# Lower parts of the first four up-projection weights on DVE, and modulation work behind the last token transpose

## The chip, the cores and the metric

The kernel runs on one core of a Trainium2 chip. Its time is device microseconds of one execution, and the number compared is the median of the runs. PE is the matrix engine (PEld its weight loads), DVE the vector engine, ACT the scalar engine, POOL the general engine, and SP the engine that issues most of the loads.

## The reference

512 tokens of 1024 features pass through two blocks. The first adds an attention mix and then an MLP with squared ReLU; the second is modulated by a condition vector:

```python
x = x + jnp.einsum('bse,ed->bsd', mixed, w_out)            # first block
hn = rmsnorm(x, mlp_norm_g)
hid = jnp.square(jax.nn.relu(jnp.einsum('bsd,df->bsf', hn, w_up)))
x = x + jnp.einsum('bsf,fd->bsd', hid, w_down)
...
mod_x = (jax.nn.silu(c) @ w_mod[l] + b_mod[l])[:, None, :] # second block
mod_c = jax.nn.silu(c_ctx) @ w_mod[l] + b_mod[l]
...                                                        # pooling and neighbourhood attention -> mix_x
x = x + gt1 * _rmsnorm(mix_x, g_post_mix[l])
y_x = _sq_relu_mlp(_modulate(x, g_pre_mlp[l], sh2, sc2), w_mlp_in[l], w_mlp_out[l])
x = x + gt2 * _rmsnorm(y_x, g_post_mlp[l])
```

All of it is float32. `w_mod` is 1024 x 6144; its product with two vectors (the condition and that of the context) gives the six modulation rows. The hidden width of both MLPs is 4096.

## The kernel before, in words

Every float32 operand of a large product is held as two parts: hi, a rounded copy that ACT writes, and lo, the source less hi, which DVE (or POOL, where `eng` says so) subtracts. That pair of instructions is `split`, lines 147 and 148. `mm3` (lines 152 to 154) forms hi x hi, hi x lo and lo x hi. A lo part is therefore always behind its hi part, and the third of three matmuls needs it.

The stages that the change touches:

- The output projection of the first block, which works off the four token tiles. `evac1` adds the residual (`xa`, line 938), multiplies by the norm's gain (`xg`, line 940), and `split_T` has PE transpose the tile (line 216, `n_0t` to `n_3t`) and splits the result into `hT`, the right-hand side of the first MLP. Tokens 0 and 1 and then 2 and 3 form the two 256-column halves in which the first up-projections run (`m1up`, weights `m1u0`, `m1u1`, ...).
- The first MLP, `mlp`. `up(j)` takes a 128-column weight of `w_up` through `weights`, which loads it (raw ring `m1u`) and splits it into `m1u{j}h` and `m1u{j}l`, both 128x1024, in a ring of five. For j below `WPJ` = 4 POOL does the lo part (line 829), for all others DVE. The squared ReLU of the result is `m1re`, `m1sq`, `m1hid`.
- The modulation, `mods`, a generator that `mlp` advances through `extra` after each up-projection. For each of six column blocks it loads eight 128x1024 tiles of `w_mod` on SP's queue (line 893) into two buffers (`mod`), and for each tile DVE multiplies it by one column of the condition and accumulates: line 896 for the first of the eight, line 898 for the other seven. Blocks 0 and 1 do that for both vectors, so each tile has a pair of instructions there. The accumulated tile `macc` is split into `mh` and `ml`, and PE sums it over the partitions with a matrix of ones (`mp`, lines 910 and 911).
- The output projection of the second block, `dense_two`. `evac1` there writes `y` (line 1265), `post` adds it to the tokens (`xb`, line 1244, scaled by `ssy` that POOL computes), `mod_T` scales (`n_0x` to `n_3x`, line 232), transposes, applies the modulation (`n_0v` to `n_3v`, lines 241 and 243) and splits into `h2T`.
- The second MLP, `mlp_seven`, whose `up` (line 1317) has the same rule for its weights `m2u0` to `m2u3`.

A scheduler in the build sets the order of the instructions on each engine from the data dependences, its own model of durations and the order in which the code issues them. The engines then run their lists in order; an instruction that waits holds up all behind it on its engine.

Of the kernel before, what the change touches and what calls it, by code (L numbers as in the profile page):

```python
# [16 lines left out]
P = 128  # L17
# [3 lines left out]
KC = D // P  # L21
# [73 lines left out]
RB2 = 2  # L95
RBX = (1, 1)
KPS2 = (2, 0, 1, 3)
WPJ = 4
LOP = 0
OT = True  # L100
DT = False
# [28 lines left out]
class Build:  # L130
# [14 lines left out]
    def split(self, hi, lo, src, eng=None):  # L145

        self.nc.scalar.activation(out=hi, in_=src, func=AF.Copy)  # L147
        (eng or self.nc.vector).tensor_tensor(out=lo, in0=src, in1=hi.bitcast(F32), op=ALU.subtract)  # L148

    def mm3(self, out, lh, ll, rh, rl, start, stop):  # L150
        mm = self.nc.tensor.matmul
# [670 lines left out]
    def mlp(self, hT, w1, w2, evac, extra, name, G=8):  # L822

        nc = self.nc
        ac = nc.scalar.activation
        hq = {}

        def up(j):
            wh, wl = self.weights(f"{name}u{j}", [(0, self.kview(w1, 0, KC, j * P, P))], KC, P, eng=self.nc.gpsimd if j < WPJ else None)
            acc = self.ps("s", f"{name}up{j}")  # L830
            nsp = 2 if j < NSP else 1
            w = SEQ // nsp
            if j % 4 == 0:
                hq[j // 4] = self.hquad(f"{name}hid{j // 4}")
            qd = hq[j // 4]
            for sp in range(nsp):
                cols = slice(sp * w, (sp + 1) * w)
                for k in range(KC):
                    hqd = hT[k // 4]
                    self.mm3(acc[:, cols], wh[:, k, :], wl[:, k, :], hqd[:, k % 4, 0, cols], hqd[:, k % 4, 1, cols], k == 0, k == KC - 1)  # L840
            r = self.ep.tile([P, SEQ], F32, tag="relu", name=f"{name}re{j}", bufs=2)
            s = self.ep.tile([P, SEQ], F32, tag="sqr", name=f"{name}sq{j}", bufs=2)
            ac(out=r, in_=acc, func=AF.Relu)  # L843
            nc.vector.scalar_tensor_tensor(out=s, in0=acc, scalar=0.0, in1=r, op0=ALU.max, op1=ALU.mult)  # L844
            self.split(qd[:, j % 4, 0, :], qd[:, j % 4, 1, :], s)
# [24 lines left out]
    def mods(self):  # L870

        nc, a = self.nc, self.a
        ac = nc.scalar.activation
        ep = self.ep
        sc = ep.tile([P, 2, KC], F32, tag="silu", name="silu_c", bufs=1)
        se = ep.tile([P, 2, KC], F32, tag="silue", name="silu_e", bufs=1)
        nc.gpsimd.dma_start(out=sc[:, 0, :], in_=a["c_2"][0].rearrange("(k p) -> p k", p=P))
        nc.gpsimd.dma_start(out=sc[:, 1, :], in_=a["c_ctx_2"].rearrange("(k p) -> p k", p=P))
        ac(out=se, in_=sc, func=AF.Exp, scale=-1.0)
        nc.vector.tensor_scalar(out=se, in0=se, scalar1=1.0, scalar2=None, op0=ALU.add)  # L880
        nc.vector.reciprocal(out=se, in_=se)
        nc.vector.tensor_tensor(out=sc, in0=sc, in1=se, op=ALU.mult)
        ones = ep.tile([P, P], F32R, tag="ones", name="ones", bufs=1)
        nc.vector.tensor_scalar(out=ones, in0=self.ident, scalar1=0.0, scalar2=1.0, op0=ALU.mult, op1=ALU.add)

        todo = {0: [(0, None, 1), (1, None, 7)], 1: [(0, "g_pre_mix_2", 0), (1, "g_pre_mix_2", 6)], 2: [(0, "g_post_mix_2", 2)],
                3: [(0, None, 4)], 4: [(0, "g_pre_mlp_2", 3)], 5: [(0, "g_post_mlp_2", 5)]}
        yield
        for cb in range(6):
            accs = [ep.tile([P, D], F32, tag=f"macc{s}", name=f"macc{cb}{s}", bufs=1) for s, _, _ in todo[cb]]  # L890
            for k in range(KC):
                rw = ep.tile([P, D], F32, tag="mraw", name=f"mod{cb}{k}", bufs=2)
                nc.sync.dma_start(out=rw, in_=a["w_mod_2"][0, k * P:(k + 1) * P, cb * D:(cb + 1) * D])
                for s in range(len(accs)):
                    if k == 0:
                        nc.vector.tensor_scalar(out=accs[s], in0=rw, scalar1=sc[:, s, k:k + 1], scalar2=None, op0=ALU.mult)
                    else:
                        nc.vector.scalar_tensor_tensor(out=accs[s], in0=rw, scalar=sc[:, s, k:k + 1], in1=accs[s],  # L898
                                                       op0=ALU.mult, op1=ALU.add)
                yield  # L900
            for (s, gname, dst) in todo[cb]:
                ah = self.part("wh", f"mh{cb}{s}")
                al = self.part("wl", f"ml{cb}{s}")
                self.split(ah, al, accs[s])
                row = ep.tile([P, D], F32, tag="xr", name=f"mrow{cb}{s}", bufs=2)[0:1, :]
                nc.gpsimd.dma_start(out=row, in_=a["b_mod_2"][:, cb * D:(cb + 1) * D])
                for hf in range(2):
                    pt = self.ps("t", f"mp{cb}{s}{hf}")
                    cols = slice(hf * 512, hf * 512 + 512)
                    nc.tensor.matmul(out=pt, lhsT=ones, rhs=ah[:, cols], start=True, stop=False)  # L910
                    nc.tensor.matmul(out=pt, lhsT=ones, rhs=al[:, cols], start=False, stop=True)
                    nc.vector.tensor_tensor(out=row[:, cols], in0=pt[0:1, :], in1=row[:, cols], op=ALU.add)
                if gname:
                    gr = ep.tile([P, D], F32, tag="xr", name=f"grow{cb}{s}", bufs=2)[0:1, :]
                    nc.gpsimd.dma_start(out=gr, in_=a[gname])
                    nc.vector.scalar_tensor_tensor(out=row, in0=row, scalar=(1.0 if cb in (1, 4) else 0.0),  # L916
                                                   in1=gr, op0=ALU.add, op1=ALU.mult)
                nc.gpsimd.dma_start(out=self.modrows[dst:dst + 1, :], in_=row)  # L918
                yield
# [4 lines left out]
    def dense_one(self):  # L924
        nc, a = self.nc, self.a
# [10 lines left out]
        def evac1(half, t, acc):  # L936
# [5 lines left out]
            if half == 1:  # L942
                self.inv_rms(x[t], r2, t, f"r2_{t}", self.ep.tile([P, D], F32, tag="xr", name=f"xs{t}", bufs=2))
                nc.gpsimd.tensor_tensor(out=r2[:, t:t + 1], in0=r2[:, t:t + 1], in1=r2[:, t:t + 1], op=ALU.mult)
        self.out_proj(a["w_out"], self.mixT, evac1, "o1")
        self.banks(a=(0, 1, 2), t=(3, 4), s=(5, 6, 7))

        self.kc = self.xc.tile([P, 4, 2, 256], F32R, name="kc")
# [39 lines left out]
        for i in range(4):  # L988
            wh, wl = self.weights(f"wkc{i}", [(0, self.kview(w_in, 0, KC, 1024 + i * P, P))], KC, P)
# [288 lines left out]
    def mlp_seven(self, hT, w1, w2, y, gg, name):  # L1278
# [3 lines left out]
        nc = self.nc  # L1282
# [29 lines left out]
        def plain(j):  # L1312

            return hid[j % G // 2][:, j % 2 * 1024:j % 2 * 1024 + 1024].rearrange("p (x t) -> p x t", x=2)

        def up(j, st):
            wh, wl = self.weights(f"{name}u{j}", [(0, self.kview(w1, 0, KC, j * P, P))], KC, P, eng=nc.gpsimd if j < WPJ else None)
            acc = self.ps("s", f"{name}up{j}")
            nsp = 2 if j < NSP else 1
            w = SEQ // nsp  # L1320
            for sp in range(nsp):
                cols = slice(sp * w, (sp + 1) * w)
                for k in range(KC):
                    hqd = hT[k // 4]
                    self.mm3(acc[:, cols], wh[:, k, :], wl[:, k, :], hqd[:, k % 4, 0, cols], hqd[:, k % 4, 1, cols], k == 0, k == KC - 1)
            s = st[:, j % 2]
            ac(out=s, in_=acc, func=AF.Relu)
            nc.vector.scalar_tensor_tensor(out=s, in0=acc, scalar=0.0, in1=s, op0=ALU.max, op1=ALU.mult)  # L1328
            if j // G == NG - 1:
                self.split(plain(j)[:, 0], plain(j)[:, 1], s)  # L1330
            elif j % 2 == 0:
                hi, lo = parts_of(j % G // 2)
                self.split(hi[:, 0], lo[:, 0], s[:, 0:256])
# [77 lines left out]
        for half in range(2):  # L1411
# [8 lines left out]
            j = (NG - 1) * G  # L1420
# [30 lines left out]
```

## Time and profile before

| | us |
|---|---|
| median of 3 runs | 1255.92 |
| lowest, highest | 1253.18, 1258.51 |
| the profiled execution | 1260.07 |
| its span in the trace | 1258.3 |

Its mean granted clock of PE was 0.988 of full speed. The busy shares over the span are PE 96%, DVE 67%, ACT 45%, POOL 28%. A share is an average over stages with different limits; what a change at one place is worth is read from the timeline there. In a timeline the bracket at the end of a row is the time that the engine sat idle before the instruction, and what ended it. Rows with x2 or more join instructions of one kind that follow each other.

### The profile page before, as it was taken

How to read it: one execution, taken by the hardware profiler on the slowest of the kernel's cores; microseconds unless marked ns; L12 is line 12 of the kernel's file. 1: busy time of each engine (PE TensorE's matmuls, PEld its weight loads, DVE VectorE, ACT ScalarE, POOL GpSimd, SP SyncE). 2: the span in 40 equal slices, each digit the busy share in tenths (PEclk: the TensorE clock that was granted, in tenths of full speed). 3: DMA queues.
4: the chain of work that ended last, by engine and by line, in shares of the span. 5: the costliest groups of instructions: out<-in, count | busy, mean ns of one | idle time of the engine just before them, and what ended most of it. 6: DMA issues, size and time to landing. Idle time of an engine off the chain costs nothing. (4 is left out here: it accounts for less than half of the span.)

```text
span 1258.3 us, 16992 instructions
## 1 busy us (share of the span) xinstructions
PE 1213.5 (96%) x6316; PEld 1017.5 (81%) x6316; DVE 844.6 (67%) x1410; ACT 567.3 (45%) x1068; POOL 355.1 (28%) x370
## 2 busy tenths in 40 slices
PE   7899999999999999999999999999899999999997
PEld 6898888779888878888889878777798888888885
DVE  3799766597898854346355557574868678777744
ACT  5576656434223313225254546463546454343431
POOL 2787552252010000000014124030642504205502
PEclk9899999999999999999999999999999999999999
DMA  6222222365678734134145311215443643524421
GB/s 165 64 60 53 57 63 68 101 183 154 197 220 258 240 119 138 67 101 135 67 151 157 84 53 52 85 38 201 124 162 102 185 123 117 147 81 134 150 68 67
DMA packets 151707, 150.71 MB, mean 120 GB/s; under 512 B 14345, under 2 KB 115480, under 8 KB 151624
## 3 DMA queue, kind: packets, MB, share of 16 engines
q1 hardware_dynamic: 147224, 139.41, 36.4%
q0 software_dynamic: 4400, 10.22, 2.6%
q8 instruction: 49, 0.80, 0.3%
q14 instruction: 34, 0.28, 0.1%
HBM read 143.24 MB, written 6.36 MB: 119 GB/s over the span
## 5 line engine op out<-in xcount | busy, mean ns | idle before, releaser
L1365 POOL TENSOR_TENSOR m2d<-m2d,m2d 128x1024 f32<-128x1024 f32 x24 | 71.2, 2981 | 162.2 <-DVE m2w220l L148 51.5
L898 DVE SCALAR_TENSOR_TENSOR macc<-mod,silu_c,macc 128x1024 f32<-128x1024 f32 x56 | 76.1, 1369 | 15.5 <-DMA mod<-in_w_mod_dram 15.2
L975 DVE SCALAR_TENSOR_TENSOR xa<-m1d,r,xa 128x512 f32<-128x512 f32 x32 | 23.8, 746 | 37.5 <-PE m1d L154 37.5
L918 POOL DMA_DIRECT2D modrows<-mrow x8 | 3.9, 492 | 146.4 <-DVE mrow L916 91.9
L147 ACT ACTIVATE m2hid<-m2sq 128x512 fp32r<-128x512 f32 (+1 forms) x32 | 17.6, 551 | 49.1 <-DVE m2sq L1328 49.1
L147 ACT ACTIVATE m1hid<-m1sq 128x512 fp32r<-128x512 f32 x32 | 20.0, 630 | 38.3 <-DVE m1sq L844 38.3
L148 DVE TENSOR_TENSOR npl<-t,nph 128x512 fp32r<-128x512 f32 x32 | 21.7, 682 | 16.4 <-ACT nph L147 16.3
L194 POOL TENSOR_SCALAR p<-p,d 128x512 f32<-128x512 f32 x8 | 14.0, 1752 | 57.1 <-DVE d L1116 27.3
L148 DVE TENSOR_TENSOR m2hid<-m2sq,m2hid 128x512 fp32r<-128x512 f32 (+1 forms) x32 | 24.3, 760 | 6.0 <-ACT m2hid L147 5.8
L181 POOL TENSOR_SCALAR w<-w,g_attn 128x384 f32<-128x384 f32 x20 | 25.8, 1297 | 9.1 <-DMA w<-in_w_in_dram 6.7
L148 DVE TENSOR_TENSOR m1hid<-m1sq,m1hid 128x512 fp32r<-128x512 f32 x32 | 22.0, 687 | 9.1 <-ACT m1hid L147 9.1
L683 DVE TENSOR_REDUCE mb<-sb 128x1 f32<-128x128 f32 (+3 forms) x32 | 15.6, 487 | 16.5 <-PE sb L680 16.4
L1115 ACT ACTIVATE p<-s,m 128x512 f32<-128x512 f32 x32 | 22.0, 688 | 5.8 <-DVE m L1113 5.8
L1069 POOL TENSOR_TENSOR tb<-G,nam 128x256 f32<-128x256 f32 x24 | 17.8, 774 | 22.1 <-DVE m L1109 12.5
L685 ACT ACTIVATE pb<-sb,mb 128x128 f32<-128x128 f32 (+3 forms) x32 | 16.8, 525 | 16.0 <-DVE mb L683 15.7
L843 ACT ACTIVATE m1re<-m1up 128x512 f32<-128x512 f32 x32 | 18.6, 583 | 10.1 <-PE m1up L154 9.8
L204 POOL TENSOR_SCALAR nc_0ss<-nc_0ss 128x1 f32<-128x1 f32 x1 | 0.2, 187 | 80.5 <-ACT nc_0x L256 80.5
L152 PE MATMUL pj<-w_0h,xnT 128*128 128x384 f32 (+1 forms) x48 | 18.0, 376 | 4.9 <-ACT pjs L407 3.9
L147 ACT ACTIVATE nph<-t 128x512 fp32r<-128x512 f32 x32 | 19.0, 595 | 7.5 <-PE t L1126 7.2
L981 POOL DMA_DIRECT2D xspill<-xa x4 | 2.6, 655 | 70.0 <-DVE xa L975 69.9
L844 DVE SCALAR_TENSOR_TENSOR m1sq<-m1up,m1re 128x512 f32<-128x512 f32 x32 | 21.8, 683 | 0.1
L1328 DVE SCALAR_TENSOR_TENSOR m2sq<-m2up,m2sq 128x512 f32<-128x512 f32 x32 | 21.9, 684 | 0.0
(2017 smaller groups left out, 4679.7 us busy)
## 6 DMA issues: line engine op xcount, KB each, us to landing
mod<-in_w_mod_dram SPq DMA_DIRECT2D x48, 512.0 KB, 4.6
m2d<-in_w_mlp_out_dram SPq DMA_DIRECT2D x44, 512.0 KB, 3.7
m1u<-in_w_up_dram SPq DMA_DIRECT2D x32, 512.0 KB, 4.3
m1d<-in_w_down_dram SPq DMA_DIRECT2D x32, 512.0 KB, 3.6
m2u<-in_w_mlp_in_dram SPq DMA_DIRECT2D x32, 512.0 KB, 4.1
w<-in_w_in_dram SPq DMA_DIRECT2D x16, 512.0 KB, 4.2
w<-in_w_in_dram SPq DMA_DIRECT2D x48, 128.0 KB, 2.6
o1w<-in_w_out_dram SPq DMA_DIRECT2D x8, 512.0 KB, 3.8
```

Of the source, the lines that this page charges most:

```text
L147: self.nc.scalar.activation(out=hi, in_=src, func=AF.Copy)
L148: (eng or self.nc.vector).tensor_tensor(out=lo, in0=src, in1=hi.bitcast(F32), op=ALU.subtract)
L152: mm(out=out, lhsT=lh, rhs=rh, start=start, stop=False)
L181: eng.tensor_scalar(out=rv[:, i], in0=rv[:, i], scalar1=g, scalar2=None, op0=ALU.mult)
L843: ac(out=r, in_=acc, func=AF.Relu)
L844: nc.vector.scalar_tensor_tensor(out=s, in0=acc, scalar=0.0, in1=r, op0=ALU.max, op1=ALU.mult)
L898: nc.vector.scalar_tensor_tensor(out=accs[s], in0=rw, scalar=sc[:, s, k:k + 1], in1=accs[s], op0=ALU.mult, op1=ALU.add)
L975: nc.vector.scalar_tensor_tensor(out=x[t][:, cols], in0=acc, scalar=r2[:, t:t + 1], in1=x[t][:, cols], op0=ALU.mult, op1=ALU.add)
L1069: nc.gpsimd.tensor_tensor(out=tb[:, h, y], in0=G[:, h, ::-1, o:o + 32][:, :, ::-1], in1=nam[:, y, :].unsqueeze(1).to_broadcast([P, 8, 32]) ...
L1115: ac(out=pr, in_=s, func=AF.Exp, bias=m[:, 2:3], accum_out=den[:, 0:1])
L1328: nc.vector.scalar_tensor_tensor(out=s, in0=acc, scalar=0.0, in1=s, op0=ALU.max, op1=ALU.mult)
L1365: pt(out=o, in0=x, in1=z, op=ALU.subtract)
```

## The change

It has two parts. In both MLPs the rule that gave the lo parts of the first four weights to POOL is gone, so that DVE subtracts all of them. And in `mods`, the two instructions of column block 0 that multiply the first tile are issued behind `turned_in`, the last `split` of the first output projection, which is the lo part of token tile 3 in `hT`. Issued behind means that the scheduler may not place them ahead of it on DVE; the accumulations that follow depend on them and so move as well.

```diff
@@ -95,7 +95,6 @@
 RB2 = 2
 RBX = (1, 1)
 KPS2 = (2, 0, 1, 3)
-WPJ = 4
 LOP = 0
 OT = True
 DT = False
@@ -145,7 +144,7 @@
     def split(self, hi, lo, src, eng=None):
 
         self.nc.scalar.activation(out=hi, in_=src, func=AF.Copy)
-        (eng or self.nc.vector).tensor_tensor(out=lo, in0=src, in1=hi.bitcast(F32), op=ALU.subtract)
+        self.last_split = (eng or self.nc.vector).tensor_tensor(out=lo, in0=src, in1=hi.bitcast(F32), op=ALU.subtract)
 
     def mm3(self, out, lh, ll, rh, rl, start, stop):
         mm = self.nc.tensor.matmul
@@ -826,7 +825,7 @@
         hq = {}
 
         def up(j):
-            wh, wl = self.weights(f"{name}u{j}", [(0, self.kview(w1, 0, KC, j * P, P))], KC, P, eng=self.nc.gpsimd if j < WPJ else None)
+            wh, wl = self.weights(f"{name}u{j}", [(0, self.kview(w1, 0, KC, j * P, P))], KC, P)
             acc = self.ps("s", f"{name}up{j}")
             nsp = 2 if j < NSP else 1
             w = SEQ // nsp
@@ -893,7 +892,8 @@
                 nc.sync.dma_start(out=rw, in_=a["w_mod_2"][0, k * P:(k + 1) * P, cb * D:(cb + 1) * D])
                 for s in range(len(accs)):
                     if k == 0:
-                        nc.vector.tensor_scalar(out=accs[s], in0=rw, scalar1=sc[:, s, k:k + 1], scalar2=None, op0=ALU.mult)
+                        with self.tc.issue_after(self.turned_in.ins) if cb == 0 else nullcontext():
+                            nc.vector.tensor_scalar(out=accs[s], in0=rw, scalar1=sc[:, s, k:k + 1], scalar2=None, op0=ALU.mult)
                     else:
                         nc.vector.scalar_tensor_tensor(out=accs[s], in0=rw, scalar=sc[:, s, k:k + 1], in1=accs[s],
                                                        op0=ALU.mult, op1=ALU.add)
@@ -943,6 +943,8 @@
                 self.inv_rms(x[t], r2, t, f"r2_{t}", self.ep.tile([P, D], F32, tag="xr", name=f"xs{t}", bufs=2))
                 nc.gpsimd.tensor_tensor(out=r2[:, t:t + 1], in0=r2[:, t:t + 1], in1=r2[:, t:t + 1], op=ALU.mult)
         self.out_proj(a["w_out"], self.mixT, evac1, "o1")
+
+        self.turned_in = self.last_split
         self.banks(a=(0, 1, 2), t=(3, 4), s=(5, 6, 7))
 
         self.kc = self.xc.tile([P, 4, 2, 256], F32R, name="kc")
@@ -1314,7 +1316,7 @@
             return hid[j % G // 2][:, j % 2 * 1024:j % 2 * 1024 + 1024].rearrange("p (x t) -> p x t", x=2)
 
         def up(j, st):
-            wh, wl = self.weights(f"{name}u{j}", [(0, self.kview(w1, 0, KC, j * P, P))], KC, P, eng=nc.gpsimd if j < WPJ else None)
+            wh, wl = self.weights(f"{name}u{j}", [(0, self.kview(w1, 0, KC, j * P, P))], KC, P)
             acc = self.ps("s", f"{name}up{j}")
             nsp = 2 if j < NSP else 1
             w = SEQ // nsp
```

At the entry of the first MLP this stands in DVE's list before: the accumulations of the last two tiles of column block 0 among the token work (`xa`, `xg`, `hT` as above; `o` the projection's result).

```order
L898 SCALAR_TENSOR_TENSOR macc_3459<-mod_3668,silu_c,macc_3459 128x1024
L898 SCALAR_TENSOR_TENSOR macc_3460<-mod_3668,silu_c,macc_3460 128x1024
L940 TENSOR_TENSOR xg_3329<-xa_3022,g_mlp 128x512
L898 SCALAR_TENSOR_TENSOR macc_3459<-mod_3734,silu_c,macc_3459 128x1024
L898 SCALAR_TENSOR_TENSOR macc_3460<-mod_3734,silu_c,macc_3460 128x1024
L148 TENSOR_TENSOR hT_3031<-n_1t_3290,hT_3031 128x4x128
L938 TENSOR_TENSOR xa_3023<-o_3_3344,xa_3023 128x512
L148 TENSOR_TENSOR hT_3031<-n_2t_3331,hT_3031 128x4x128
L940 TENSOR_TENSOR xg_3370<-xa_3023,g_mlp 128x512
L148 TENSOR_TENSOR m1u4l<-m1u_3672,m1u4h 128x1024
L148 TENSOR_TENSOR hT_3031<-n_3t_3372,hT_3031 128x4x128
L148 TENSOR_TENSOR ml_3739<-macc_3459,mh_3738 128x1024
```

In the list now, at the same place, with block 0's first accumulations at the end:

```order
L147 TENSOR_TENSOR m1u1l<-m1u_3465,m1u1h 128x1024
L147 TENSOR_TENSOR m1u2l<-m1u_3534,m1u2h 128x1024
L938 TENSOR_TENSOR xa_3023<-o_3_3344,xa_3023 128x512
L940 TENSOR_TENSOR xg_3370<-xa_3023,g_mlp 128x512
L147 TENSOR_TENSOR hT_3031<-n_2t_3331,hT_3031 128x4x128
L147 TENSOR_TENSOR m1u3l<-m1u_3603,m1u3h 128x1024
L147 TENSOR_TENSOR m1u4l<-m1u_3672,m1u4h 128x1024
L147 TENSOR_TENSOR hT_3031<-n_3t_3372,hT_3031 128x4x128
L896 TENSOR_SCALAR macc_3459<-mod_3461,silu_c 128x1024
L896 TENSOR_SCALAR macc_3460<-mod_3461,silu_c 128x1024
L898 SCALAR_TENSOR_TENSOR macc_3459<-mod_3526,silu_c,macc_3459 128x1024
L898 SCALAR_TENSOR_TENSOR macc_3460<-mod_3526,silu_c,macc_3460 128x1024
```

What moved: the accumulations stand behind the last `hT` lo part, and the lo parts `m1u1l`, `m1u2l` and `m1u3l`, which were not in DVE's list, stand ahead of it. Between the last transposes `n_3t` and the first sum `mp` PE's list has 210 matmuls of 256 columns now, and had 177 before.

PE's list at the first sums of the modulation, before (`mp` with its two halves of columns, and up-projection 5 behind):

```order
L154 MATMUL m1up_3678<-hT_3031,m1u4l 128x256
L910 MATMUL mp_3744<-mh_3738,ones 128x512
L911 MATMUL mp_3744<-ml_3739,ones 128x512
L910 MATMUL mp_3748<-mh_3738,ones 128x512
L911 MATMUL mp_3748<-ml_3739,ones 128x512
L152 MATMUL m1up_3759<-hT_3030,m1u5h 128x512
L153 MATMUL m1up_3759<-hT_3030,m1u5h 128x512
```

And now:

```order
L153 MATMUL m1up_3678<-hT_3031,m1u4l 128x256
L910 MATMUL mp_3744<-mh_3738,ones 128x512
L910 MATMUL mp_3748<-mh_3738,ones 128x512
L151 MATMUL m1up_3759<-hT_3030,m1u5h 128x512
L152 MATMUL m1up_3759<-hT_3030,m1u5h 128x512
L911 MATMUL mp_3744<-ml_3739,ones 128x512
L911 MATMUL mp_3748<-ml_3739,ones 128x512
L151 MATMUL m1up_3817<-hT_3030,m1u6h 128x512
L152 MATMUL m1up_3817<-hT_3030,m1u6h 128x512
L153 MATMUL m1up_3759<-hT_3030,m1u5l 128x512
```

What moved: the two sums of `mh` come first, two matmuls of `m1up` with `m1u5h` stand between them and the sums of `ml`, and the first matmul with `m1u5l` follows two more with `m1u6h`.

DVE's list at the entry of the second MLP, before:

```order
L232 TENSOR_SCALAR n_0x<-xb_8441,ssx_8550 128x1024
L1244 SCALAR_TENSOR_TENSOR xb_8442<-y_8424,ssy_8435,xb_8442 128x512 x2
L1265 TENSOR_TENSOR y_8425<-o_2_8684,g_post 128x512
L243 TENSOR_SCALAR n_0v_8580<-n_0t_8575,g_mod_8429 128x128 x4
L232 TENSOR_SCALAR n_1x<-xb_8442,ssx_8647 128x1024
L148 TENSOR_TENSOR h2T_8432<-n_0v_8568,h2T_8432 128x4x128
L148 TENSOR_TENSOR h2T_8433<-n_0v_8580,h2T_8433 128x4x128
L1265 TENSOR_TENSOR y_8425<-o_2_8714,g_post 128x512
L243 TENSOR_SCALAR n_1v_8677<-n_1t_8672,g_mod_8429 128x128 x4
L148 TENSOR_TENSOR h2T_8432<-n_1v_8665,h2T_8432 128x4x128
L148 TENSOR_TENSOR h2T_8433<-n_1v_8677,h2T_8433 128x4x128
L1244 SCALAR_TENSOR_TENSOR xb_8443<-y_8425,ssy_8436,xb_8443 128x512 x2
```

And now, from `n_0v` on (`m2u0l` and `m2u1l` stand ahead of these rows):

```order
L242 TENSOR_SCALAR n_0v_8580<-n_0t_8575,g_mod_8429 128x128 x4
L231 TENSOR_SCALAR n_1x<-xb_8442,ssx_8647 128x1024
L147 TENSOR_TENSOR m2u2l<-m2u_9013,m2u2h 128x1024
L147 TENSOR_TENSOR h2T_8432<-n_0v_8568,h2T_8432 128x4x128
L147 TENSOR_TENSOR h2T_8433<-n_0v_8580,h2T_8433 128x4x128
L147 TENSOR_TENSOR m2u3l<-m2u_9072,m2u3h 128x1024
L1267 TENSOR_TENSOR y_8425<-o_2_8714,g_post 128x512
L242 TENSOR_SCALAR n_1v_8677<-n_1t_8672,g_mod_8429 128x128 x4
L1246 SCALAR_TENSOR_TENSOR xb_8443<-y_8425,ssy_8436,xb_8443 128x512 x2
L147 TENSOR_TENSOR m2u4l<-m2u_9138,m2u4h 128x1024
L147 TENSOR_TENSOR h2T_8432<-n_1v_8665,h2T_8432 128x4x128
L147 TENSOR_TENSOR h2T_8433<-n_1v_8677,h2T_8433 128x4x128
```

What moved: `m2u2l` stands ahead of the first token's `h2T` lo parts, and `m2u3l`, the pair `xb` of token tile 2 and `m2u4l` ahead of the second token's, where that pair and `m2u4l` were behind it.

## Rows read from the trace of the kernel before

**Rows 1.** Page, part 1: busy us (share of the span) xcount.
```profile
PE 1213.5 (96%) x6316; PEld 1017.5 (81%) x6316; DVE 844.6 (67%) x1410; ACT 567.3 (45%) x1068; POOL 355.1 (28%) x370
```

**Rows 2.** Timeline of PE, first MLP's entry: start, us, engine, line, op, idle before.
```profile
284.77 0.63 PE L216 MATMUL n_2t<-ident,xg 128*128 128x128 f32 x4 [3.15 <-DVE xg L940]
...
291.49 0.60 PE L216 MATMUL n_3t<-ident,xg 128*128 128x128 f32 x4
```

**Rows 3.** Windows: stretch, PE, PEld, DVE, ACT, POOL busy, granted clock, DMA share, GB/s.
```profile
285.00:289.00 4.00, 4.00 (x24) 4.00 (x23) 4.00 (x6) 1.43 (x3) 3.92 (x3) 0.57 1.03 292
296.00:345.00 49.00, 49.00 (x283) 42.95 (x283) 42.80 (x48) 18.95 (x26) 2.87 (x5) 1.00 0.55 165
345.00:420.00 75.00, 75.00 (x324) 60.69 (x323) 63.27 (x67) 22.66 (x27) 8.21 (x14) 1.00 0.75 236
446.00:449.00 3.00, 3.00 (x9) 2.32 (x8) 2.46 (x3) 1.30 (x2) 0.00 (x0) 0.50 0.26 101
906.00:910.00 4.00, 3.99 (x21) 3.99 (x22) 3.72 (x5) 3.51 (x10) 1.24 (x4) 0.59 0.17 62
```

**Rows 4.** Timeline of DVE, entry of the first MLP.
```profile
278.33 5.69 DVE L898 SCALAR_TENSOR_TENSOR macc<-mod,silu_c,macc 128x1024 f32<-128x1024 f32 x2
...
284.54 2.47 DVE L898 SCALAR_TENSOR_TENSOR macc<-mod,silu_c,macc 128x1024 f32<-128x1024 f32 x2
...
292.75 0.69 DVE L148 TENSOR_TENSOR hT<-n_3t,hT 128x512 fp32r<-128x512 f32 x1 [0.92 <-ACT hT L147]
...
306.59 0.75 DVE L896 TENSOR_SCALAR macc<-mod,silu_c 128x1024 f32<-128x1024 f32 x1
```

**Rows 5.** Timeline of POOL, the same stretch.
```profile
279.60 3.34 POOL L148 TENSOR_TENSOR m1u2l<-m1u,m1u2h 128x1024 fp32r<-128x1024 f32 x1
```

**Rows 6.** Timeline of PE, entry of the second MLP.
```profile
898.03 1.06 PE L216 MATMUL n_1t<-ident,n_1x 128*128 128x128 f32 x8 [1.35 <-DVE n_1x L232]
...
904.14 0.38 PE L152 MATMUL m2up<-h2T,m2u3h 128*128 128x256 f32 x1 [0.63 <-DVE y L1265]
906.01 0.39 PE L153 MATMUL m2up<-h2T,m2u1h 128*128 128x256 f32 x1 [1.49 <-DVE h2T L148]
```

**Rows 7.** Timeline of DVE, entry of the second MLP.
```profile
888.14 5.69 DVE L1244 SCALAR_TENSOR_TENSOR xb<-y,ssy,xb 128x512 f32<-128x512 f32 x2 [0.43 <-POOL ssy L1237]
895.26 0.69 DVE L1265 TENSOR_TENSOR y<-o,g_post 128x512 f32<-128x512 f32 x1 [1.42 <-ACT sj L1232]
...
898.12 5.37 DVE L148 TENSOR_TENSOR h2T<-n_0v,h2T 128x512 fp32r<-128x512 f32 x2 [0.23 <-ACT h2T L147]
...
906.66 1.41 DVE L1244 SCALAR_TENSOR_TENSOR xb<-y,ssy,xb 128x512 f32<-128x512 f32 x2
907.99 1.22 DVE L148 TENSOR_TENSOR m2u4l<-m2u,m2u4h 128x1024 fp32r<-128x1024 f32 x1
...
917.06 1.29 DVE L148 TENSOR_TENSOR h2T<-n_2v,h2T 128x512 fp32r<-128x512 f32 x2
```

**Rows 8.** Loads of line 893: issue to landing of 512 KB, us.
```profile
DMA to landing us min/median/max: 3.6/4.6/9.2
```

**Rows 9.** Timeline of PE, up to the first sums of the modulation.
```profile
307.23 0.28 PE L152 MATMUL m1up<-hT,m1u4h 128*128 128x256 f32 x1
...
312.93 0.39 PE L910 MATMUL mp<-mh,ones 128*128 128x512 f32 x1
313.16 0.40 PE L911 MATMUL mp<-ml,ones 128*128 128x512 f32 x1
```

**Rows 10.** Page, part 5: multiply-adds of line 898: count, busy, mean ns, idle before them.
```profile
L898 DVE SCALAR_TENSOR_TENSOR macc<-mod,silu_c,macc 128x1024 f32<-128x1024 f32 x56 | 76.1, 1369 | 15.5 <-DMA mod<-in_w_mod_dram 15.2
```

**Rows 11.** Timeline of all engines at a later sum of the modulation.
```profile
422.26 1.06 ACT L147 ACTIVATE mh<-macc 128x1024 fp32r<-128x1024 f32 x1 [2.18 <-DVE macc L898]
...
424.79 0.40 PE L911 MATMUL mp<-ml,ones 128*128 128x512 f32 x1
```

**Rows 12.** Timeline of PE, a wait for DVE later in the first MLP.
```profile
444.42 0.50 PE L152 MATMUL m1d<-m1d100h,m1hid 128*128 128x512 f32 x1 [1.81 <-DVE xa L975]
```

## The prediction

> **What bounds the kernel now.** I read the busy table first: PE is busy for 1213.5 of 1258.3 us, DVE for 844.6, POOL for 355.1 [rows 1]. So the time is PE's list, and work that moves between DVE and POOL counts only where PE waits for it, or where PE's clock is lower after such a wait. The second view is therefore PE's timeline at the two places the change touches. At the entry of the first MLP PE stands 3.15 us ahead of the transposes `n_2t`, until DVE has written `xg` [rows 2], and the stretch from 285 to 289 shows a granted clock of 0.57, near the 1.2 GHz level, against 1.00 at 2.4 GHz [rows 3]. At the entry of the second MLP it stands 1.35, 0.63 and 1.49 us, each time for DVE, and 906 to 910 shows 0.59 [rows 3, 6]. Third, DVE's timeline there. In the first MLP a pair of accumulations took 5.69 us where the next pair took 2.47 [rows 4]; in its time POOL ran `m1u2l`, 279.60 to 282.94 [rows 5]. In the second, one `xb` pair took 5.69 us and a later one 1.41, one `h2T` pair 5.37 and a later one 1.29 [rows 7]. The reader should see that DVE is not full but late, and that its slow pairs lie beside POOL's lo parts.
>
> **The change part by part.** Durations are of the execution of 1260.07 us (span 1258.3, and 1.8 around it), which lies 4.15 above the median of 1255.92. The sum is a difference, made there and carried to the median.
>
> *A, first entry.* The last `xg` no longer stands behind the slow pair: the accumulations are out of the token work, and POOL has no lo part to run beside it. What comes in is `m1u1l` to `m1u3l`, each 1.22 us by the row of `m2u4l` [rows 7]; one of them costs half of the pair that it replaces, so DVE is early for `xg`. The wait of 3.15 goes, and with it the low clock, 4 us x (1 - 0.57) = 1.7. Together -4.9. Bounds: 0, if lo parts that wait for ACT's hi parts hold `xg` as long, and -4.9.
>
> *B, second entry.* The waits are 1.35 + 0.63 + 1.49 = 3.47, the clock 4 x (1 - 0.59) = 1.6. On DVE 5.69 - 1.41 = 4.28 and 5.37 - 1.29 = 4.08 go. Five lo parts and an `xb` pair now stand ahead of the second token's `h2T` parts: 5 x 1.22 + 1.41 = 7.5. So these come 0.9 earlier if all stands back to back, and 2.9 if the lo parts fill the idle 0.43 + 1.42 + 0.23 [rows 7]. I take the middle, 1.9, and half of the clock, 0.8: -2.7. Bounds: -5.1, all waits and clock gone, and 0: the `xb` pair that is now ahead waits for POOL's `ssy`, and behind it on DVE are `m2u4l` and the `h2T` parts that PE waits for; a wait like the 0.43 in front of the pair at 888.14, twice, would take back the 0.9.
>
> *C, first sums of the modulation.* The moved accumulations now start behind the lo part of `n_3t`, which ended 292.75 + 0.69 - 291.49 = 1.95 us after the transposes began [rows 2, 4]. Two tiles are loaded by then; each later load starts only when one of the two buffers is free. With the median landing of 4.6 us [rows 8], 2.47 for a pair and 1.4 for the first pair (two of 0.75 that overlap a little) [rows 4]: tiles 0 and 1 are done at 1.4 and 3.9; tile 2 lands at 6.0 and is done at 8.5; tile 3 lands at 8.5, done at 11.0; tile 4 at 15.6, tile 5 at 18.1, tile 6 at 22.7, tile 7 at 25.2, the first vector's half of it at 24.0. ACT's hi part `mh` takes 1.06 [rows 11]. From the transposes: 1.95 + 24.0 + 1.06 = 27.0. The `m1sq` and `m1hid` instructions of the up-projections that stand between the pairs fit in the load waits in part; up to 1.9 more, or 28.9. What covers it on PE are the 210 matmuls of 256 columns between the transposes and the first sum. 48 such took 312.93 - 307.23 = 5.70 us [rows 9], so 24.9, and 0.4 for the transposes: 25.3. The new wait is 1.7 to 3.6; I take 2.7. The sums of `ml` and the first matmul with `m1u5l` follow one and two DVE lo parts behind; four and two matmuls at 0.23 [rows 9] lie between: 1.22 - 0.9 + 1.22 - 0.5 = 1.0. Behind a wait of this length the clock has been low (A), 1.7 more. C = +5.4. Queued behind the waiting `mp` is all of the first MLP, since PE's list is one line. Bounds: 0, where landings at the shortest, 3.6, take 3 x 1.0 off the chain (three load cycles stand in it); and 10.0, where one of them is the longest, 9.2.
>
> By the Trainium skill ("DMA: Bandwidth & Descriptors", "Anatomy of one DMA", fitted on the gpsimd path) a transfer takes about 2.0 us plus its bytes at 436 GB/s, an estimate of 3.2 us for 512 KB. By that figure C would be nothing and the sum -2.5; the trace does not agree, with 3.6 as its shortest landing and 4.6 as its median, under other traffic.
>
> *D, the later sums.* 2.47 x 7 + 1.4 = 18.7 us of DVE work moves behind 293. DVE was idle for 49.00 - 42.80 + 75.00 - 63.27 = 17.9 between 296 and 420 [rows 3], and 15.2 of the idle time before accumulations in the whole kernel was spent on loads [rows 10], which a later DVE no longer waits for. So it nearly fits, but with no room left: at the sum near 424.6 `mh` ended at 422.26 + 1.06, a lo part of 1.22 behind it ends at 424.54, and PE took `ml` at 424.79: 0.2 us to spare [rows 11]. Of four sums in this stretch (column blocks 1 to 4) I take two to be late by as much as the nearest wait for DVE, 1.81 [rows 12], and one of them with the clock that followed that wait, 3 x (1 - 0.50) = 1.5 [rows 3]: 5.1. Bounds: 0, and four times 1.81 + 1.5, 13.2. What leaves POOL beyond A and B is idle time there and worth nothing: in these rows only the `xb` pair waits for POOL, for `ssy`, which comes no later with less ahead of it.
>
> Sum: -4.9 - 2.7 + 5.4 + 5.1 = +2.9. Profiled 1263.0; on the median 1255.92 + 2.9 = 1258.8.
>
> **The rivals.** *Faster: the modulation stays hidden.* If loads land near 3.6 us, C is nothing and DVE reaches the later sums with its old lead: -7.6 with D at 0, -10.0 with B at its bound. For it: idle time of 17.9 for 18.7 of work, and the lead that block 0 had before: its accumulations stood ahead of the lo part at 292.75, 20 us ahead of the first sum at 312.93 [rows 4, 9]. Against it: 4.6 is the median, and the chain goes through three landings in a row. Time 1246 to 1248.
>
> *Slower: modulation sets PE's time through the whole first MLP.* One mechanism: each column block starts where the one before ends, through two buffers, so a delay at the first sums is passed on, and every sum stalls PE and lowers its clock. It decides from the point at which `mh` is over 5 us late at the first sum. Landings 1 us longer give C 5.4 + 3.0 = 8.4; three late sums with their clock give D 3 x 3.31 = 9.9; less 7.6, that is +10.7: 1266.6. For it: the 0.2 us to spare, and that PE works in a single line. Against it: the idle time of DVE.
>
> *The slow pairs were not POOL's doing*, or the new lo parts hold `xg` as long: A is 0 and B is 0, C and D stay, +10.5, 1266.4. Against it: the excess of the slow pair, 5.69 - 2.47 = 3.22, is the length of the POOL lo part in its time, 3.34 [rows 4, 5]. It is in the chance of slower, with 0.04.
>
> **How the numbers follow.** This kernel's measurement tells no change from 0.5%, that is 6.3 us. Forecast, within 1249.6 to 1262.2: 0.49, with its own range 1253 to 1262. The faster rival 0.19; slower, both mechanisms, 0.32, since C and D have more room upward (10.0 and 13.2) than A and B downward. The 80% range takes in both rivals' times: 1247.5 to 1268.
>
> **What would show it.** A: no wait over 0.5 us at `n_2t`, and a clock of 1.00 behind it. B: PE's waits at the second entry sum to 1 to 2.5 us in place of 3.47, no `xb` or `h2T` pair above 1.6 us. C: a wait of 1.7 to 3.6 us at the first `mp<-mh`, released by ACT, and tiles of the modulation that land one after the other ahead of it. D: two waits near 1.8 us at later sums or at `m1` lo parts. The forecast is wrong if C's wait is missing (then faster), or if sums 2 to 5 each show a wait (then slower).

## The result and the profile after

The changed kernel takes 1263.87 us (median of 8 runs) against 1256.57 of the kernel before (8 runs). One run of the changed kernel took 4145.91 us and is left out of the ratio; the median of the other seven is 1263.56. The ratio is 1.0051, with a 95% interval of 1.0035 to 1.0066: slower by about 6.4 us. The profiled execution took 1263.56 us (span 1261.5), 3.5 more than the profiled execution of before, which at 1260.07 was above every one of the eight runs of before (1258.71 at the most). So the two profiles show about half of the change, and what follows places only that half.

Where it went is read by following single matmuls of PE through both traces. These are starts in us, and what the changed kernel is ahead (-) or behind (+) there:

| PE starts | before | after | difference | in this stretch |
|---|---|---|---|---|
| last `o1w00h`, ahead of the first entry | 247.99 | 245.59 | -2.40 | -2.4 |
| last `m1u4h`, just ahead of the first sum | 312.69 | 305.47 | -7.22 | A: -4.8 |
| last `m1u7h`, behind the first sums | 331.05 | 331.03 | -0.02 | C: +7.2 |
| first `m1u16h`, behind the sum of block 4 | 474.98 | 480.50 | +5.52 | D: +5.5 |
| last transposes of `p` in the attention | 842.71 | 849.62 | +6.91 | +1.4 |
| first `m2u5h`, behind the second entry | 937.69 | 940.94 | +3.25 | B: -3.7 |

The letters are the parts of the prediction. The first and the fifth stretch hold nothing of the change; the last section says what they are. In the rows of PE the wait of 3.15 at `n_2t` [rows 2] is gone, and three waits for `mh` stand where before there was none:

```profile
280.35 0.60 PE L215 MATMUL n_3t<-ident,xg 128*128 128x128 f32 x4
...
310.04 1.22 PE L910 MATMUL mp<-mh,ones 128*128 128x512 f32 x2 [4.17 <-ACT mh L146]
...
312.48 1.22 PE L911 MATMUL mp<-ml,ones 128*128 128x512 f32 x2 [0.27 <-DVE ml L147]
...
404.75 0.73 PE L910 MATMUL mp<-mh,ones 128*128 128x512 f32 x2 [1.74 <-ACT mh L146]
...
431.34 1.22 PE L910 MATMUL mp<-mh,ones 128*128 128x512 f32 x2 [2.54 <-ACT mh L146]
...
910.76 0.39 PE L152 MATMUL m2up<-h2T,m2u1h 128*128 128x256 f32 x1 [1.74 <-DVE h2T L147]
```

The waits in brackets belong to C (4.17 and 0.27), to D (1.74 and 2.54) and to what is left of B: one of 1.74 where 1.35, 0.63 and 1.49 stood [rows 6]. The windows at the same places (granted clock is the third number from the right):

```profile
281.00:285.00 4.00, 4.00 (x36) 4.00 (x35) 3.52 (x5) 1.45 (x2) 1.09 (x2) 1.00 0.47 136
310.00:316.00 6.00, 5.69 (x14) 3.83 (x15) 6.00 (x7) 3.35 (x4) 0.00 (x0) 0.57 0.54 165
430.00:440.00 10.00, 8.66 (x31) 6.68 (x32) 9.48 (x12) 5.13 (x6) 0.00 (x0) 0.83 0.65 222
910.00:916.00 6.00, 5.24 (x44) 5.25 (x45) 4.70 (x8) 2.38 (x8) 3.89 (x7) 1.00 0.95 299
```

The first entry runs at 1.00, where it had 0.57 [rows 3]; the low level has moved to the stretches behind the sums, 0.57 and 0.83. DVE at the first entry, in the changed kernel:

```profile
276.55 0.69 DVE L938 TENSOR_TENSOR xa<-o,xa 128x512 f32<-128x512 f32 x1 [0.47 <-PE o L153]
277.27 0.69 DVE L940 TENSOR_TENSOR xg<-xa,g_mlp 128x512 f32<-128x512 f32 x1
...
280.30 1.23 DVE L147 TENSOR_TENSOR m1u3l<-m1u,m1u3h 128x1024 fp32r<-128x1024 f32 x1 [1.73 <-ACT m1u3h L146]
282.00 1.23 DVE L147 TENSOR_TENSOR m1u4l<-m1u,m1u4h 128x1024 fp32r<-128x1024 f32 x1 [0.47 <-ACT m1u4h L146]
283.14 0.68 DVE L147 TENSOR_TENSOR hT<-n_3t,hT 128x512 fp32r<-128x512 f32 x1
283.74 1.40 DVE L896 TENSOR_SCALAR macc<-mod,silu_c 128x1024 f32<-128x1024 f32 x2
...
290.80 2.48 DVE L898 SCALAR_TENSOR_TENSOR macc<-mod,silu_c,macc 128x1024 f32<-128x1024 f32 x2 [3.26 <-DMA mod<-in_w_mod_dram]
...
309.42 1.28 DVE L898 SCALAR_TENSOR_TENSOR macc<-mod,silu_c,macc 128x1024 f32<-128x1024 f32 x1
```

`xg` follows 0.03 us behind `xa` and is no longer late. But the lo parts `m1u3l` and `m1u4l` wait for ACT's hi parts, 1.73 and 0.47 us, ahead of the lo part of `n_3t`, so the accumulations begin 3.39 us after the transposes (283.74 - 280.35), and the last of block 0's ends at 310.7. ACT in its turn had waited for the weights' loads:

```profile
279.20 1.06 ACT L146 ACTIVATE m1u3h<-m1u 128x1024 fp32r<-128x1024 f32 x1 [0.58 <-DMA m1u<-in_w_up_dram]
...
280.90 1.06 ACT L146 ACTIVATE m1u4h<-m1u 128x1024 fp32r<-128x1024 f32 x1 [0.64 <-DMA m1u<-in_w_up_dram]
```

DVE at the second entry has its short pairs back, 1.29 and 1.40 where rows of 5.37 and 5.69 stood [rows 7], and `xb` and `m2u4l` ahead of the `h2T` pair that PE waits for:

```profile
903.07 1.29 DVE L147 TENSOR_TENSOR h2T<-n_0v,h2T 128x512 fp32r<-128x512 f32 x2 [0.43 <-ACT h2T L146]
...
907.56 1.40 DVE L1246 SCALAR_TENSOR_TENSOR xb<-y,ssy,xb 128x512 f32<-128x512 f32 x2
908.89 1.21 DVE L147 TENSOR_TENSOR m2u4l<-m2u,m2u4h 128x1024 fp32r<-128x1024 f32 x1
910.02 1.28 DVE L147 TENSOR_TENSOR h2T<-n_1v,h2T 128x512 fp32r<-128x512 f32 x2
```

### The profile page after: what moved, and what is told of

It is laid out like the page before. It is cut to its first block, busy times and chain, and to the rows that moved or that the text cites. A ratio compares the mean times of both kernels' runs of the same rounds, so it can differ in the third digit from the quotient of the medians.

```text
span 1261.5 us, 16987 instructions
## 1 busy us (share of the span) xinstructions
PE 1211.4 (96%) x6316; PEld 1011.5 (80%) x6316; DVE 841.7 (67%) x1418; ACT 568.1 (45%) x1068; POOL 326.5 (26%) x362
## 5 line engine op out<-in xcount | busy, mean ns | idle before, releaser
L1367 POOL TENSOR_TENSOR m2d<-m2d,m2d 128x1024 f32<-128x1024 f32 x24 | 68.0, 2844 | 166.7 <-DVE m2w120l L147 52.8
L898 DVE SCALAR_TENSOR_TENSOR macc<-mod,silu_c,macc 128x1024 f32<-128x1024 f32 x56 | 70.6, 1275 | 18.7 <-DMA mod<-in_w_mod_dram 18.7
L146 ACT ACTIVATE mh<-macc 128x1024 fp32r<-128x1024 f32 x8 | 8.4, 1055 | 31.2 <-DVE macc L898 29.2
```

Source lines behind the costliest of these rows:

```text
L1367: pt(out=o, in0=x, in1=z, op=ALU.subtract)
```

## The experiments

All ratios are to the kernel before, with 95% intervals.

**The lo parts alone.** The order behind `turned_in` is taken out again:

```diff
-                        with self.tc.issue_after(self.turned_in.ins) if cb == 0 else nullcontext():
+                        with nullcontext():
```

> Only the lo parts move to DVE, in both MLPs; block 0 of the modulation keeps its place among the token work. My theory (the delay at the modulation's sums is made by the second part alone, and the slow pairs by POOL's lo parts): no accumulation pair above 2.6 us at the first entry, the 3.15 us wait at n_2t falls under 1 us, no wait at any mp, the second entry gains about 2 us as in the changed kernel; 5 to 7 us below before, about 1250, ratio 0.994 to 0.996. Rival 1 (DVE is full at the entry, the lo parts now stand ahead of xg beside the accumulations): the wait at n_2t stays at 2 to 4 us, ratio 0.998 to 1.000. Rival 2 (four more lo parts on DVE are what makes the sums late): waits of 2 to 4 us at mp remain, ratio 1.002 or more.

1254.92 us, 0.9992 [0.9979, 1.0005]. DVE and PE, in this kernel:

```profile
278.52 2.47 DVE L898 SCALAR_TENSOR_TENSOR macc<-mod,silu_c,macc 128x1024 f32<-128x1024 f32 x2
280.91 1.22 DVE L147 TENSOR_TENSOR m1u2l<-m1u,m1u2h 128x1024 fp32r<-128x1024 f32 x1
282.05 0.68 DVE L940 TENSOR_TENSOR xg<-xa,g_mlp 128x512 f32<-128x512 f32 x1
```

```profile
283.41 0.38 PE L151 MATMUL m1up<-hT,m1u3h 128*128 128x256 f32 x1 [1.28 <-ACT m1u3h L146]
...
399.69 0.74 PE L910 MATMUL mp<-mh,ones 128*128 128x512 f32 x2 [1.57 <-ACT mh L146]
```

The pair of accumulations is back at 2.47 us with no lo part on POOL beside it, and `xg` is in time; the first sums wait for nothing. So the wait at `n_2t` goes without moved accumulations, and it was POOL's lo parts that stretched DVE. A new wait of 1.28 us for the hi part of `m1u3` stands behind it, so from 247 to the first sum PE gains 3.2 us here, not 4.8. And a later sum is late by 1.57 (and one by 0.59), although block 0 kept its place. My expected 0.994 to 0.996 is missed by these waits. Rival 2 has the later sums late, as they are, but its waits of 2 to 4 us and its ratio of 1.002 did not come. By its interval this kernel can't be told from the kernel before.

**The order alone.** The changed kernel with POOL's lo parts put back in both MLPs (`up` of each has the second of these edits):

```diff
+WPJ = 4
...
-            wh, wl = self.weights(..., KC, P)
+            wh, wl = self.weights(..., KC, P, eng=self.nc.gpsimd if j < WPJ else None)
```

> Only block 0's accumulations are issued behind the last hT lo part; POOL keeps the lo parts of the first four weights in both MLPs. My theory: the first entry loses most of its wait (nothing long of DVE stands ahead of xg, though POOL's lo parts can still stretch an xg or hT part by up to 2.4 us), -3 to -5 us; waits at the first sum of 3 to 5 us and at two later ones as in the changed kernel, +12 to +13; the second entry as before: 7 to 10 us above before, ratio 1.006 to 1.008. Rival (the lo parts on DVE make the sums late): under 1 us at the first sum, ratio 0.996 to 0.999.

1270.07 us, 1.0103 [1.0084, 1.0123].

```profile
311.31 1.22 PE L911 MATMUL mp<-mh,ones 128*128 128x512 f32 x2 [4.30 <-ACT mh L147]
...
407.75 0.73 PE L911 MATMUL mp<-mh,ones 128*128 128x512 f32 x2 [2.72 <-ACT mh L147]
...
912.37 0.39 PE L152 MATMUL m2up<-h2T,m2u3h 128*128 128x256 f32 x1 [0.61 <-DVE y L1268]
914.24 0.39 PE L153 MATMUL m2up<-h2T,m2u1h 128*128 128x256 f32 x1 [1.48 <-DVE h2T L148]
```

The wait at the first sum is 4.30 with none of the first MLP's lo parts moved to DVE: C is the order's doing. PE's gain from 247 to the first sum is 4.8 us here too (-1.30 at the last `o1w00h`, -6.08 at the last `m1u4h`). Either half of the change takes A's wait away; the second half pays C for it. The second entry keeps its waits of before. In the profiles C is 7.0 us here and D 6.3, together about the 12 to 13 that I expected at the sums, and this profiled execution is 6.9 us above that of before. By the ratio the kernel is 12.9 us slower, more than expected. The profiles do not show where the rest lies: the one here is the fastest of five runs, and that of before is a slow one.

**The second MLP alone.** Only the line of `mlp_seven` changes, the first MLP is that of before.

> Only the second MLP's first four lo parts move to DVE; the first MLP and the modulation are as before. My theory: the second entry alone, waits of 3.5 us and the low clock turn into one wait of about 1.7 us: -2 us, ratio 0.998 to 0.999, and the first entry shows the 3.15 us wait and the slow pair again. Rival (POOL's lo parts were not what stretched DVE's pairs): no change, ratio 1.000, pairs of 5 us stay.

1254.06 us, 0.9981 [0.9963, 0.9999].

```profile
282.34 0.63 PE L216 MATMUL n_2t<-ident,xg 128*128 128x128 f32 x4 [3.29 <-DVE xg L940]
...
899.74 0.39 PE L153 MATMUL m2up<-h2T,m2u1h 128*128 128x256 f32 x1 [1.69 <-DVE h2T L148]
```

As expected: one wait of 1.69 is left at the second entry, 3.29 stays at the first. B is real and is worth about 0.2%.

**Six loads fewer for block 0.** The changed kernel, with block 0 on its first two tiles, which it multiplies four times in turn; its other six loads are left out:

```diff
+                if cb == 0 and k >= 2:
+                    rw = kept[k % 2]
+                else:
+                    rw = ep.tile([P, D], F32, tag="mraw", name=f"mod{cb}{k}", bufs=2)
...
+                kept = {**(kept if k else {}), k % 2: rw}
```

> The changed kernel, but block 0 of the modulation loads only its first two tiles and multiplies them four times in turn, so that its accumulations wait for no load (six of 48 loads are left out). If the loads through two buffers set the time of the first sum, as my prediction's working of C had it: DVE idles no more between 284 and 309, where it idled 3.8 us, the wait of 4.17 us at the first mp falls to under 0.5 us, and the later sums come on time too; 3 to 5 us below before, ratio 0.996 to 0.998. Rival (DVE's list itself is the pace, 18.7 us of accumulations with m1sq, m1hid between them): 1.5 to 4 us of the wait stay, ratio 1.001 to 1.004.

1261.75 us, 1.0046 [1.0030, 1.0061]. PE, and the page's group of accumulations:

```profile
308.97 0.74 PE L914 MATMUL mp<-mh,ones 128*128 128x512 f32 x2 [1.69 <-ACT mh L146]
...
404.72 0.81 PE L914 MATMUL mp<-mh,ones 128*128 128x512 f32 x2 [2.94 <-ACT mh L146]
```

```profile
L902 DVE SCALAR_TENSOR_TENSOR macc<-mod,silu_c,macc 128x1024 f32<-128x1024 f32 x56 | 70.7, 1275 | 15.2 <-DMA mod<-in_w_mod_dram 15.2
```

At the first sum 2.5 of 4.17 us go: that part was the loads, and 1.69 is DVE's own list. But the sum near 404 is 2.94 us late, though block 0 waited for no load, and accumulations still wait 15.2 us for loads, none of it in block 0. My expectation is missed; the rival's time is near (1.0046 lies just above it), and its reason, DVE's list, explains the first sum only. It left this to try: each later block is itself as slow as its eight loads through two buffers. Three accumulations of block 3 in the changed kernel, around 400:

```profile
396.94 1.28 DVE L898 SCALAR_TENSOR_TENSOR macc<-mod,silu_c,macc 128x1024 f32<-128x1024 f32 x1 [2.20 <-DMA mod<-in_w_mod_dram]
...
398.75 1.28 DVE L898 SCALAR_TENSOR_TENSOR macc<-mod,silu_c,macc 128x1024 f32<-128x1024 f32 x1
402.32 1.28 DVE L898 SCALAR_TENSOR_TENSOR macc<-mod,silu_c,macc 128x1024 f32<-128x1024 f32 x1 [2.30 <-DMA mod<-in_w_mod_dram]
```

Two of three wait over 2 us for their tile.

**Three buffers.** The changed kernel with a third buffer for the modulation's tiles. There was no room for it, so the first MLP squares its ReLU in place:

```diff
-            s = self.ep.tile([P, SEQ], F32, tag="sqr", name=f"{name}sq{j}", bufs=2)
-            nc.vector.scalar_tensor_tensor(out=s, in0=acc, scalar=0.0, in1=r, op0=ALU.max, op1=ALU.mult)
-            self.split(qd[:, j % 4, 0, :], qd[:, j % 4, 1, :], s)
+            nc.vector.scalar_tensor_tensor(out=r, in0=acc, scalar=0.0, in1=r, op0=ALU.max, op1=ALU.mult)
+            self.split(qd[:, j % 4, 0, :], qd[:, j % 4, 1, :], r)
...
-                rw = ep.tile([P, D], F32, tag="mraw", name=f"mod{cb}{k}", bufs=2)
+                rw = ep.tile([P, D], F32, tag="mraw", name=f"mod{cb}{k}", bufs=3)
```

> The changed kernel with three buffers for the modulation's tiles instead of two; room is made by writing the first MLP's squared ReLU in place of the ReLU. After the run without six loads, where the later sums stayed late though block 0 was done without loads, my theory for the later sums is: each column block is one chain of eight loads through two buffers, some 27 to 29 us a block, as long as PE takes between two sums, so lateness is never made up. With a third buffer a block takes under 24 us: no wait over 0.5 us at the sums near 404 and 431, 5 us less there, and at the first sum a wait of 1.5 to 2.5 us; in all 5 to 8 us less than the changed kernel, ratio to before 0.998 to 1.001. Rival (DVE's list is full, the order decides): the waits at the later sums stay within 1 us of 1.7 and 2.5, ratio 1.004 to 1.006.

1255.36 us, 0.9978 [0.9959, 0.9996], at the lower edge of what was expected.

```profile
310.39 0.74 PE L909 MATMUL mp<-mh,ones 128*128 128x512 f32 x2 [1.69 <-ACT mh L146]
```

```profile
L897 DVE SCALAR_TENSOR_TENSOR macc<-mod,silu_c,macc 128x1024 f32<-128x1024 f32 x56 | 70.3, 1273 | 2.1 <-DMA mod<-in_w_mod_dram 2.1
```

No later sum waits any more: of the waits of PE over 0.25 us between 232 and 480, the 1.69 shown is the only one for a sum. Accumulations wait 2.1 us for loads where they waited 18.7:

```profile
L898 DVE SCALAR_TENSOR_TENSOR macc<-mod,silu_c,macc 128x1024 f32<-128x1024 f32 x56 | 70.6, 1275 | 18.7 <-DMA mod<-in_w_mod_dram 18.7
```

The accumulations' own work is the same (70.3 and 70.6 us), so DVE had the room all along; the chain of loads was late. The first accumulations of block 2 and of block 5, in the changed kernel and in this one, give the length of a block:

```profile
350.89 0.75 DVE L896 TENSOR_SCALAR macc<-mod,silu_c 128x1024 f32<-128x1024 f32 x1
...
433.59 0.75 DVE L896 TENSOR_SCALAR macc<-mod,silu_c 128x1024 f32<-128x1024 f32 x1
```

```profile
349.47 0.75 DVE L895 TENSOR_SCALAR macc<-mod,silu_c 128x1024 f32<-128x1024 f32 x1
...
424.40 0.75 DVE L895 TENSOR_SCALAR macc<-mod,silu_c 128x1024 f32<-128x1024 f32 x1
```

That is 27.6 us a block with two buffers and 25.0 with three, from nearly the same start. And 1.69 at the first sum is what DVE's list costs when loads do not.

**The control.** The changed kernel with the in-place write and two buffers.

> The changed kernel with the squared ReLU of the first MLP written in place of the ReLU, and two buffers as in the change: the control for the three buffers. Both theories: as the changed kernel, ratio to before 1.003 to 1.007, waits of 4.2, 1.7 and 2.5 us at the sums. If the in-place write itself moved the sums, it would show here.

1262.83 us, 1.0048 [1.0030, 1.0066]: as the changed kernel, with waits at the same three sums.

```profile
310.83 1.22 PE L909 MATMUL mp<-mh,ones 128*128 128x512 f32 x2 [4.89 <-ACT mh L146]
...
405.28 0.73 PE L909 MATMUL mp<-mh,ones 128*128 128x512 f32 x2 [0.87 <-ACT mh L146]
...
432.21 1.22 PE L909 MATMUL mp<-mh,ones 128*128 128x512 f32 x2 [2.88 <-ACT mh L146]
```

One by one they differ by up to 0.9 us from those of the changed kernel (4.17, 1.74, 2.54); their sum is 8.6 and 8.5.

**The lo parts alone, with three buffers.** Both edits above, without the order.

> Only the lo parts on DVE (no issue behind), with three buffers for the modulation's tiles and the ReLU squared in place. By the theory of the chain of loads: the later sums, 1.57 and 0.59 us late with the lo parts alone, come on time, block 0's accumulations stay early, both entries keep their gain: 7 to 10 us below before, ratio 0.992 to 0.995. Rival (order on DVE): waits at the later sums stay, ratio 0.998 to 1.000.

1248.97 us, 0.9925 [0.9903, 0.9947]: faster than both kernels. The waits of PE at the two entries, and none over 0.25 at any sum:

```profile
283.80 0.39 PE L151 MATMUL m1up<-hT,m1u3h 128*128 128x256 f32 x1 [0.67 <-ACT m1u3h L146]
...
897.33 0.39 PE L152 MATMUL m2up<-h2T,m2u1h 128*128 128x256 f32 x1 [1.58 <-DVE h2T L147]
```

**The second MLP alone, with three buffers.**

> Only the second MLP's lo parts on DVE, with three buffers for the modulation's tiles and the ReLU squared in place; POOL keeps the first MLP's lo parts. The 3.15 us wait at n_2t is POOL's doing and should stay within 1 us, the sums come on time: 2 to 4 us below before, ratio 0.997 to 0.999, as without the third buffer. Rival (the accumulations, with loads that come earlier, leave the token work by themselves): the wait at n_2t goes, ratio 0.993 to 0.996.

1254.38 us, 0.9975 [0.9963, 0.9988], as expected: a third buffer is worth nothing measurable where the sums were in time, and the wait at the first entry stays, now at `n_1t`:

```profile
280.01 1.08 PE L216 MATMUL n_1t<-ident,xg 128*128 128x128 f32 x4 [3.01 <-DVE xg L939]
```

**`xb` behind.** The kernel with the lo parts and three buffers, and the `xb` pair of token tile 2 behind the second token's `h2T` lo parts:

```diff
+                    with self.tc.issue_after(self.h2_in.ins) if t == 2 else nullcontext():
                         for hf, c in self.post(x[t], ...):
...
                     self.mod_T(x[t], g, hT, t, f"n4_{t}", rx)
+                    self.h2_in = self.last_split
```

> The lo parts on DVE with three buffers as in the run before that did so, and at the second entry the xb pair of token tile 2 issued behind the second token's h2T lo parts. My working of B: the remaining wait of 1.6 us at the second entry is DVE's, with xb (1.4 us) and m2u4l (1.2) ahead of those lo parts; without xb the wait falls to 0.2 to 0.6 us, 1 to 1.4 us less than that run, ratio to before 0.991 to 0.993; what could be late next are the transposes of token tile 2, 1.4 us later than they were. Rival (the lo parts wait for ACT's hi part or for the modulated token, not for the list): the wait stays at 1.2 us or more and the time is the same, ratio 0.992 to 0.994, or 0.5 to 1.5 us more by the later tile 2.

1247.78 us, 0.9920 [0.9896, 0.9945].

```profile
890.05 1.21 DVE L147 TENSOR_TENSOR m2u4l<-m2u,m2u4h 128x1024 fp32r<-128x1024 f32 x1
```

```profile
891.92 0.38 PE L152 MATMUL m2up<-h2T,m2u1h 128*128 128x256 f32 x1 [0.81 <-DVE h2T L147]
```

The wait falls from 1.58 to 0.81, so the `xb` pair held half of it, less than I expected. `m2u4l` still stands in DVE's list right ahead of the `h2T` lo parts; whether the rest of the wait is its 1.21 us was not tried. A wait of 0.27 stands at 908.10, in front of `m2up`, for ACT's `h2T` part. In the times the two kernels can't be told apart.

## Why the prediction was right, and where it was not

The forecast was +2.9 us and 1258.8; measured were 6.4 by the ratio and 1263.87. That is inside the 80% range of 1247.5 to 1268, but above the forecast's own range of 1253 to 1262, on the side to which 0.32 was given. The sign came from the right balance: two gains at the entries against two losses at the sums. In the profiles the four parts add up to +4.2, near the forecast. The other 2 to 3 us are the sum's starting point: it was made on an execution of before that was 3.5 slower than the median of eight and carried to the median as it was. That execution had low clocks worth 1.7 and 1.6 us at the two entries, which A and B counted as the kernel's; the last section shows waits as long without them. That these are the missing us in the median run is likely, and not shown, since no trace of such a run of before was kept.

- *A, -4.9 forecast, -4.8 in the profiles.* The wait and the clock are gone as said (the clock with the reserve just made), and the cause named, POOL's lo part beside the slow pair, is shown by the run with the lo parts alone. What I had not seen is that either half of the change is enough for this wait.
- *B, -2.7 forecast, -3.7 in the profiles.* The waits went from 3.47 to 1.74, where 1.9 less was taken; the low clock went altogether, not by half. The last run shows that half of the remaining wait is the `xb` pair's place.
- *C, +5.4 forecast, +7.2 in the profiles.* What PE has to do before the first sum was sized right: PE came to the first sum 25.5 us after the transposes (310.04 - 4.17 - 280.35), 25.3 forecast. So was the chain from there: `mh` began at 308.9, 25.2 us after the accumulations, with 24.0 to 25.9 worked out. Its make-up was in part another: the working has three waits of 2.1 us for loads in it, so that loads are the pace; with six loads left out it still took 22.7 (285.2 to 307.9), so DVE's list nearly fills it and the loads added 2.5. What was mis-sized is its start, 3.39 us after the transposes and not 1.95, because `m1u3l` and `m1u4l` wait for ACT in DVE's list ahead of the lo part of `n_3t`. The price of a lo part on DVE was taken as its 1.22 us, without that wait. These 1.44 us are nearly all of the difference between the wait of 2.7 forecast and the 4.17 measured. The low clock behind it cost 2.6 (6 us at 0.57), 1.7 forecast, and the sums of `ml` 0.27, 1.0 forecast. The estimate of 3.2 us for a load, from the Trainium skill ("DMA: Bandwidth & Descriptors", "Anatomy of one DMA"), would have had no wait here; in the changed kernel too the median from issue to landing is 4.6.
- *D, +5.1 forecast, +5.5 in the profiles: the right number by a wrong reason.* Two late sums were forecast, and 1.74 and 2.54 came, with 1.7 of low clock behind the second (10 us at 0.83). But the step said that 18.7 us of moved work fill DVE's idle 17.9, and that a later DVE waits less for loads. It waited more, 18.7 in place of 15.2 [rows 10]; with a third buffer the same work fits without a wait at a later sum, and without six of block 0's loads the lateness stays. What I had put into the slower rival, blocks that follow one another through two buffers, is the mechanism: from block 2 to block 5 the changed kernel takes 27.6 us a block, and the kernel before 27.9 (341.8 to 425.6); with a third buffer it is 25.0. A delay is not made up with two buffers, since PE's own distance between sums is shorter than a block (372.5, 401.3 and 424.6 before, 26.0 on average). With the third buffer block 2 begins about as late, and a block is then shorter than that distance. The rival went too far in that it had every sum stall and asked for a first sum over 5 us late: two later sums stalled, behind a first one 4.2 late.

Why the lo parts alone, with block 0 in its place, make a later sum late by 1.57 is not settled in its first cause: block 2 begins 3.4 us later there (345.2 against 341.8), and with the third buffer the lateness is gone. Which instruction starts it was not tried. That the wait at the first sum can go to nothing with the order kept was not tried either.

## What to carry to other kernels

Work taken off a crowded stretch is not free where it lands: ask what feeds it, and count its buffers there. If a chain of load, use and release takes as long per piece as its consumer leaves, it has no slack, and one delay is paid again at each later point; one more buffer cured it here, and idle time of the engine was no sign of slack. When a change has two halves that remove the same wait, try each alone: here the lo parts without the order are at 0.9992 with two buffers and 0.9925 with three, and both halves together at 1.0051 and 0.9978.

## What the runs showed of the hardware

A wait of the same length does not always lower PE's clock. At 240 us every kernel here waits 1.87 us for `mixT`. Before, and in the changed kernel, the windows show:

```profile
240.00:250.00 10.00, 8.98 (x32) 7.25 (x33) 2.27 (x5) 1.62 (x3) 3.47 (x4) 0.83 0.72 240
```

```profile
240.00:250.00 10.00, 9.86 (x45) 8.02 (x46) 3.94 (x6) 2.82 (x4) 2.62 (x3) 1.00 0.66 212
```

In the eleven profiles of this study the granted clock in that stretch was 0.83 five times and 1.00 six times. With the second MLP alone the wait of 3.29 us at the first entry was followed by a clock of 1.00 throughout, where before 3.15 was followed by 0.57:

```profile
282.00:289.00 7.00, 6.52 (x54) 6.35 (x55) 6.09 (x8) 4.08 (x6) 6.40 (x7) 1.00 0.82 241
```

At the second entry the order alone has the three waits of before (1.35, 0.61 and 1.48), and a clock of 1.00 behind the last of them, where before had 0.59 [rows 3]:

```profile
914.00:918.00 4.00, 3.76 (x31) 3.77 (x32) 3.67 (x6) 3.53 (x9) 1.02 (x3) 1.00 0.18 59
```

The clock that is missing in such a stretch, times its length, comes to 1.5 to 2.6 us in the windows here and in [rows 3]. The difference of -2.4 ahead of the first entry holds one fall. In the fifth stretch of the table it is the other way: 0.91 from 830 to 850 in the changed kernel, 1.00 before. So 1.7 of A and 1.6 of B may belong to the one execution that was profiled, and single profiles differ by some such terms; the waits at the entries come back (3.15 and 3.29, 1.49 and 1.48).

A lo part on POOL does not stretch all that DVE does beside it. Before, the pair at 284.54 took its 2.47 us [rows 4] although POOL ran `m1u3l` from 285.83 for 3.44 us, while the pair before it took 5.69.
